# Weights as the moving operand: 512-column matmuls in gates and two output projections, merged matmuls in the input projection

## The chip, the cores and the metric

The kernel runs on one core of a Trainium2 chip. The metric is the device time of one execution in microseconds (us), as the median over several runs; lower is better. Engines are named as in the profile: PE (TensorE matmul), PEld (its weight loads), DVE (VectorE), ACT (ScalarE), POOL (GpSimd), SP (SyncE, which issues most DMAs).

## The reference

One layer of an encoder trunk over 256 tokens of 2048 channels in float32, and a last RMSNorm:

```
n  = rms_norm(h);  u = n @ w_in            # columns: q, kv, rope key | z, xBC, dt | gates g_attn, g_ssd
a  = mla(u) @ w_o_attn                     # 16 heads, rotary key, softmax over 256 keys
s  = rms_norm((y_f + y_b + d * xs) * silu(z)) @ w_o_ssd     # two scans in chunks of 128, 8 groups
m  = sigmoid(g_attn) * a + sigmoid(g_ssd) * s
h  = h + m @ w_out
h  = h + conv_ffn(rms_norm(h))             # up 2 x 5632, depthwise conv over 3, gate, down
out = rms_norm(h)
```

xBC goes through a depthwise convolution over five tokens and a silu before the scans.

## The kernel before

Everything lies transposed on the chip: channels in the 128 partitions, the 256 tokens in the free dimension. The weights are cut into slabs of 128 output channels by 16 blocks of 128 input channels (1 MB each). A slab is one *job*: SP loads it into one of three `raw` buffers (`load`, L128), and each half of it (eight blocks) is split by ACT and DVE into a rounded part `wh` and a rest `wl` (`split_to`, L139 and L140), in one of HB=5 buffers each. PE multiplies the parts with the activations, which are split in the same way (hi and lo, in one page with hi in row 0 and lo in row 1), and sums over the blocks in a PSUM bank. There are four banks (`gps`, tile `g`) for the jobs and four (`sps`, tile `s`) for the rest.

Two forms of the products exist. `mm3` (L145 to L147) makes three matmuls for each block, each with 256 moving columns (the tokens) and each with its own weight load. `dense(..., merge=True)` (L165, L166) makes two: `wh` against hi and lo at once, 512 columns, into both halves of a bank, and `wl` against hi, 256 columns, into the first half:

```
if merge:
    pe.matmul(ps, lhsT=wh[:, b, :], rhs=x, start=k == 0, stop=False)
    pe.matmul(ps[:, 0, :], lhsT=wl[:, b, :], rhs=x[:, 0, :], start=False, stop=k == ktot - 1)
else:
    mm3(ps, wh[:, b, :], wl[:, b, :], x[:, 0, :], x[:, 1, :], k == 0, k == ktot - 1)
```

The halves of a merged bank are then added by `halves_sum` (an ACT copy, L178, and a DVE add, L179). A third form stands in `v_job` (L509 to L511) alone: the activations are the stationary operand (128 tokens by 128 channels) and four weight blocks side by side the moving one, 512 columns.

The jobs run in the order in which they are appended: ten of the input projection (`win`) for the attention's latents, the rope key and dt; the attention's jobs (R, V, QK) with 16 gate slabs (`ga_job`) strewn among them; 16 slabs of `w_o_attn` (`oa_evac`); for each of eight groups B, C, four x and four z slabs of the input projection with one or two gate slabs (`gate_s`); six gate slabs; 32 jobs of `w_o_ssd`, two for each of 16 output slabs (`os_evac`); 16 of `w_out`; and the feed-forward part. Small pieces of work (rope, softmax, the scans `ssd_*`) are hung before jobs by `at(slot, ...)`. The input projection's slabs other than gates (`win` with merge=False) use `mm3`; gates, `w_o_attn`, `w_o_ssd` but for its last slab, and nearly all that follows are merged.

What is done with a finished bank: the convolved slabs (`conv5`) read it with one ACT operation (L621) and four DVE operations (L624) and end in a silu (L625); z slabs with one ACT silu (L648); gates with `halves_sum` and a tanh (L598).

Of the kernel before, what the change touches and what calls it, by code (L numbers as in the profile page):

```python
# [8 lines left out]
F32 = mybir.dt.float32  # L9
# [6 lines left out]
P = 128  # L16
S = 256
# [30 lines left out]
class Job:  # L48


    def __init__(self, src, nb, mm, evac):
        self.src, self.nb, self.mm, self.evac = src, nb, mm, evac
        self.sides, self.post = [], []
        self.whole = None


@with_exitstack
def tile_bidir_hybrid_layer(ctx: ExitStack, tc, xT, pos, vec, cst, w_in, w_r, w_v, w_qk, w_oa,
# [23 lines left out]
    def f32(ap):  # L82
        return ap.bitcast(F32)
# [17 lines left out]
    def vcol(name, i=0):  # L101
        o = VOFF[name] + i
        return V[:, o:o + 1]
# [29 lines left out]
    def split_to(n):  # L133
        while hptr[0] < min(n, len(halves)):
            i, h, nb = halves[hptr[0]]
            r = raws[i][:, 8 * h:8 * h + nb, :]
            wh = wp.tile([P, 8, P], F32R, tag="wh", bufs=HB, name="wh")
            wl = wp.tile([P, 8, P], F32R, tag="wl", bufs=HB, name="wl")
            act.activation(wh[:, :nb, :], r, AF.Copy)  # L139
            dve.tensor_sub(wl[:, :nb, :], r, f32(wh[:, :nb, :]))  # L140
            hl[hptr[0]] = (wh, wl)
            hptr[0] += 1

# [5 lines left out]
    def dense(src, nb, get, evac, cell=None, k0=0, ktot=None, merge=True):  # L149

        cell = {} if cell is None else cell
        ktot = nb if ktot is None else ktot

        def mm(h, n, wh, wl):
            if k0 == 0 and h == 0:
                cell["ps"] = gpsum([P, 2, S] if merge else [P, S])
            ps = cell["ps"]  # L160
            for b in range(n):
                k = k0 + 8 * h + b
                x = get(k)
# [11 lines left out]
        return j  # L175

    def halves_sum(ps, o):
        act.activation(o, ps[:, 1, :], AF.Copy)  # L178
        dve.tensor_add(o, o, ps[:, 0, :])  # L179
# [150 lines left out]
    def lat_evac(which, m):  # L330
        def ev(ps):
            if m == 0:
                lat[which] = page([P, 4, S], name=which)
                lat[which + "s"] = p1(name=which + "s")
            sq = lat[which + "s"] if m == 0 else p1(name="sq1")
            act.activation(lat[which][:, m, :], ps, AF.Copy)
            act.activation(sq, ps, AF.Square)
            if m:
                dve.tensor_add(lat[which + "s"], lat[which + "s"], sq)
        return ev  # L340
# [102 lines left out]

    def kr_evac(ps):
        t = p1((P, 1, S), name="krf")
        act.activation(t[:, 0, :], ps, AF.Copy)
        dts["krf"] = (t, swapped(t, 1))

    def kr_rope():
# [139 lines left out]

    ta, ts_ = {}, {}  # L590

    def gate_evac(store, m):
        def ev(ps):
            if m % 4 == 0:
                store[m // 4] = page([P, 4, S], name="gate")
            t = store[m // 4][:, m % 4, :]
            halves_sum(ps, t)
            act.activation(t, t, AF.Tanh, scale=0.5)  # L598
        return ev

    mixD = dr.tile([4, P, 4, S], F32, name="mixD")

    def oa_evac(m):
        def ev(ps):
            t = ta[m // 4]
            o = p1(name="oa")
            halves_sum(ps, o)
            dve.scalar_tensor_tensor(t[:, m % 4, :], t[:, m % 4, :], 1.0, o, ALU.add, ALU.mult)
            if m % 4 == 3:
                nc.sync.dma_start(mixD[m // 4], t)  # L610
        return ev


    class Grp:
# [3 lines left out]
    ssd_ss = {}  # L618

    def conv5(ps, cb, o):  # L620
        act.activation(o, ps, AF.Identity, scale=vcol("cw", 2 * 48 + cb), bias=vcol("cb", cb))  # L621
        for k, a, b in ((0, slice(2, S), slice(0, S - 2)), (1, slice(1, S), slice(0, S - 1)),
                        (3, slice(0, S - 1), slice(1, S)), (4, slice(0, S - 2), slice(2, S))):
            dve.scalar_tensor_tensor(o[:, a], ps[:, b], vcol("cw", k * 48 + cb), o[:, a], ALU.mult, ALU.add)  # L624
        act.activation(o, o, AF.Silu)  # L625

    def bc_evac(g, which):
# [138 lines left out]
    def ssd_r():  # L766
        r_ssd["t"] = rsqrt_tok(token_sums([ssd_ss["a"][:, b, :] for b in range(2)]), 4096)

    def ssd_r2():
        ps = spread(r_ssd["t"])  # L770
        r_ssd["r"] = p1(name="r_ssd")
        act.activation(r_ssd["r"], ps, AF.Copy)

    def ssd_split(g):
        for b in range(2):
            t = page([P, 2, 2, S], F32R, name="yHL")
# [5 lines left out]
                                         ALU.mult, ALU.subtract)  # L782
            yHL[2 * g + b] = t

    mixS, mHL = {}, {}

    def mix_load(q):
        mixS[q] = page([P, 4, S], name="mixS")
        nc.sync.dma_start(mixS[q], mixD[q])

    def os_evac(m):
        def ev(ps):
            t = ts_[m // 4][:, m % 4, :]
            o = p1(name="ms")
            sum_times(ps, r_ssd["r"], o)
            dve.scalar_tensor_tensor(o, t, 1.0, o, ALU.add, ALU.mult)
            dve.tensor_add(o, o, mixS[m // 4][:, m % 4, :])
            if m % 2 == 0:
                mHL[m // 2] = page([P, 2, 2, S], F32R, name="mHL")
            hi, lo = mHL[m // 2][:, 0, m % 2, :], mHL[m // 2][:, 1, m % 2, :]  # L800
            act.activation(hi, o, AF.Copy)
            dve.tensor_sub(lo, o, f32(hi))
        return ev


    hp, hHL = {}, {}
# [99 lines left out]

    win_i = [0]

    def win(evac, st=nHL, merge=False):
        j = dense(w_in[win_i[0]], 16, lambda k: pair(st, k), evac, merge=merge)  # L910
        win_i[0] += 1
        return j
# [4 lines left out]
        late.append((slot, lambda: fn(*a)))  # L917

    for m in range(4):
        win(lat_evac("q", m), xHL)  # L920
    for m in range(4):
        win(lat_evac("kv", m), xHL)
    win(kr_evac)
    win(dt_evac)
    at(2, emit_xsq)
# [20 lines left out]
    at(50, dt_rows)  # L946

    ga = [0]

    def ga_job():  # L950
        win(gate_evac(ta, ga[0]), merge=True)
        ga[0] += 1


# [34 lines left out]
    for it in "g R0 g g g V0 QK0 g QK1 V1 QK2 g QK3 V2 R1 g QK4 g QK5 V3 QK6 g QK7 g g g g g".split():  # L989
# [5 lines left out]
            Vj(int(it[1]))  # L995
        else:
            QK(int(it[2]))
    for m in range(16):
        dense(w_oa[m], 16, lambda k: pair(oT, k), oa_evac(m))
        if ga[0] < 16:  # L1000
            ga_job()
    gs = [0]

    def gate_s(n):
        for _ in range(n):
            win(gate_evac(ts_, gs[0]), merge=True)
            gs[0] += 1
    for g in range(G):
        b = len(jobs)
# [23 lines left out]
    for g in range(G):  # L1033
        at(b - 4 + g + (2 if g > 6 else 0), ssd_split, g)
    at(b + 5, ssd_r)
    at(b + 6, ssd_r2)
    b = len(jobs)
    for m in range(16):
        cell = {}
        dense(w_os[m, 0], 16, lambda k: pair(yHL, k), os_evac(m), cell, 0, 32, m < 15)  # L1040
        dense(w_os[m, 1], 16, lambda k: pair(yHL, k), os_evac(m), cell, 16, 32, m < 15)
    for q in range(4):
        at(b + 8 * q - (1 if q else 0), mix_load, q)
    b = len(jobs)
    for m in range(16):
# [163 lines left out]
```

## Time and profile before

| | |
|---|---|
| median of three runs | 1993.49 us (1992.39 to 1993.75) |
| the profiled execution | 1994.73 us, of which the trace spans 1992.9 us |
| busy share | PE 99%, PEld 91%, DVE 74%, ACT 60% |
| granted TensorE clock, mean | 0.997 of full speed |
| from HBM | 371.91 MB read, mean 190 GB/s |

The busy time of PE counts a matmul from its start to its end, and matmuls overlap; so the distance between the starts of two matmuls tells what one costs, and not its duration. In the rows a line of the timeline gives start (us), duration (us), engine, line, operation, the tile written and those read, and the shape.

### The profile page before, as it was taken

Reading aid. Unit: us, or ns where it says so; the run is one execution under the profiler, and the core shown is the slowest. Engines: PE = TensorE matmul, PEld = TensorE weight load, DVE = VectorE, ACT = ScalarE, POOL = GpSimd, SP = SyncE. Lnnn points to the kernel's source line nnn. Section 1 sums busy time; section 2 is a strip of 40 time slices with the busy share of each in tenths; the row PEclk is TensorE's granted clock in tenths of the full one; section 3 lists DMA queues with packets and bytes.
Section 4 is the critical chain, followed back from the end, with each engine's and each line's share of the span. In section 5 each row is a group of like instructions: output and inputs, shape, how many; then the busy total and the mean of one; then the engine's idle time right before and its main releaser. Section 6 shows DMA issues by size and latency. Waiting matters only on the chain.

```text
span 1992.9 us, 32794 instructions
## 1 busy us (share of the span) xinstructions
PE 1979.4 (99%) x13204; PEld 1810.8 (91%) x13204; DVE 1471.3 (74%) x2374; ACT 1205.5 (60%) x1894; POOL 0.2 (0%) x4
## 2 busy tenths in 40 slices
PE   9999999999999999999999999999999999999997
PEld 9999988999999999999888988888888888888886
DVE  7977766768877977887756676888756777567775
ACT  6666544677878788785644445655434555335564
POOL 0000000000000000000000000000000000000000
PEclk9999999999999999999999999999999999999998
DMA  7544356666556555644556555555555555555553
GB/s 270 180 172 156 132 176 218 239 208 205 172 206 226 181 184 207 227 171 170 187 201 211 200 210 201 187 191 189 182 184 189 190 189 181 182 189 190 185 159 122
DMA packets 58425, 379.54 MB, mean 190 GB/s; under 512 B 6816, under 2 KB 7456, under 8 KB 17568
## 3 DMA queue, kind: packets, MB, share of 16 engines
q1 hardware_dynamic: 56592, 375.08, 54.1%
q10 hardware_dynamic: 1680, 2.37, 0.4%
q8 instruction: 103, 1.69, 0.3%
q14 instruction: 50, 0.41, 0.1%
HBM read 371.91 MB, written 4.33 MB: 189 GB/s over the span
## 4 chain that ended last, share of the span: by engine, by line
PE 97%; DVE 2%; DMA 0%; ACT 0%; issue 0%; ACTq 0%; SPq 0%; DVEq 0%
PE g L165 41%; PE g L166 21%; PE g L147 10%; PE g L146 10%; PE g L145 10%; PE s L727 1%; PE s L736 1%; PE s L147 0%; PE s L145 0%; PE s L146 0%; DVE wl L140 0%; PE s L709 0%; PE s L570 0%; DVE xHL L232 0%; DMA x<-in_xT 0%; PE g L509 0%
## 5 line engine op out<-in xcount | busy, mean ns | idle before, releaser
L139 ACT ACTIVATE wh<-raw 128x1024 fp32r<-128x1024 f32 (+1 forms) x670 | 700.7, 1048 | 677.2 <-PE g L165 533.6
L140 DVE TENSOR_TENSOR wl<-raw,wh 128x1024 fp32r<-128x1024 f32 (+1 forms) x670 | 808.3, 1210 | 403.8 <-ACT wh L139 395.3
L165 PE MATMUL g<-hHL,wh 128*128 128x512 f32 x1360 | 477.6, 397 | 0.0
L145 PE MATMUL g<-xHL,wh 128*128 128x256 f32 x1424 | 405.1, 285 | 0.0
L147 PE MATMUL g<-xHL,wl 128*128 128x256 f32 x1424 | 403.5, 283 | 0.9 <-DVE wl L140 0.9
L146 PE MATMUL g<-xHL,wh 128*128 128x256 f32 x1424 | 403.6, 283 | 0.2 <-DVE xHL L232 0.2
L166 PE MATMUL g<-hHL,wl 128*128 128x256 f32 x1360 | 381.9, 281 | 0.0
L165 PEld LDWEIGHTS g<-hHL,wh 128*128 128x128 f32 x1360 | 255.3, 188 | 60.6
L147 PEld LDWEIGHTS g<-xHL,wl 128*128 128x128 f32 x1424 | 272.1, 191 | 1.1 <-DVE wl L140 1.1
L146 PEld LDWEIGHTS g<-xHL,wh 128*128 128x128 f32 x1424 | 272.2, 191 | 0.4 <-DVE xHL L232 0.4
L145 PEld LDWEIGHTS g<-xHL,wh 128*128 128x128 f32 x1424 | 272.1, 191 | 0.4
L166 PEld LDWEIGHTS g<-hHL,wl 128*128 128x128 f32 x1360 | 257.5, 189 | 0.0
L165 PE MATMUL g<-aHL,wh 128*128 128x512 f32 x692 | 244.8, 399 | 0.0
L166 PE MATMUL g<-aHL,wl 128*128 128x256 f32 x692 | 194.0, 281 | 0.0
L165 PE MATMUL g<-xHL,wh 128*128 128x512 f32 x512 | 182.0, 399 | 0.0
L165 PE MATMUL g<-yHL,wh 128*128 128x512 f32 x480 | 166.5, 392 | 0.0
L165 PEld LDWEIGHTS g<-aHL,wh 128*128 128x128 f32 x692 | 130.1, 188 | 32.6 <-DVE aHL L866 0.6
L166 PE MATMUL g<-xHL,wl 128*128 128x256 f32 x512 | 143.6, 281 | 0.0
L166 PE MATMUL g<-yHL,wl 128*128 128x256 f32 x480 | 134.6, 280 | 0.0
L166 PEld LDWEIGHTS g<-aHL,wl 128*128 128x128 f32 x692 | 131.0, 189 | 0.1
L165 PEld LDWEIGHTS g<-xHL,wh 128*128 128x128 f32 x512 | 96.3, 188 | 22.5
L165 PEld LDWEIGHTS g<-yHL,wh 128*128 128x128 f32 x480 | 89.8, 187 | 19.5
(296 smaller groups left out, 2748.2 us busy)
## 6 DMA issues: line engine op xcount, KB each, us to landing
raw<-in_w_in SPq DMA_DIRECT2D x120, 1024.0 KB, 4.9
raw<-in_w_up SPq DMA_DIRECT2D x88, 1024.0 KB, 4.8
raw<-in_w_os SPq DMA_DIRECT2D x32, 1024.0 KB, 4.8
raw<-in_w_dn SPq DMA_DIRECT2D x32, 1024.0 KB, 5.0
raw<-in_w_oa SPq DMA_DIRECT2D x16, 1024.0 KB, 4.8
FB<-acsD SPq DMA_DIRECT2D x32, 512.0 KB, 7.3
raw<-in_w_out SPq DMA_DIRECT2D x16, 1024.0 KB, 4.8
raw<-in_w_dn SPq DMA_DIRECT2D x16, 768.0 KB, 4.2
```

The costliest lines, as they stand in the source:

```text
L139: act.activation(wh[:, :nb, :], r, AF.Copy)
L140: dve.tensor_sub(wl[:, :nb, :], r, f32(wh[:, :nb, :]))
L145: pe.matmul(ps, lhsT=wH, rhs=xH, start=first, stop=False)
L146: pe.matmul(ps, lhsT=wH, rhs=xL, start=False, stop=False)
L147: pe.matmul(ps, lhsT=wL, rhs=xH, start=False, stop=last)
L165: pe.matmul(ps, lhsT=wh[:, b, :], rhs=x, start=k == 0, stop=False)
L166: pe.matmul(ps[:, 0, :], lhsT=wl[:, b, :], rhs=x[:, 0, :], start=False, stop=k == ktot - 1)
L727: pe.matmul(px[j0][:, b, c * P:(c + 1) * P], lhsT=q.xw[:, 1 - c, js], rhs=q.cX[:, 1 - c, :], start=True, stop=True)
L736: pe.matmul(ps[j0][64 * hh:64 * hh + 64, b, c * P:(c + 1) * P], lhsT=q.xt[:, c, h * 64:h * 64 + 64], rhs=q.F[c][:, h, :], start=True, stop ...
```

## The change

All of it moves work between forms of the same products.

1. **Quads.** The 32 gate slabs, the 16 slabs of `w_o_attn` and the 32 jobs of `w_o_ssd` become quads, in the manner of `v_job`. A quad is four slabs side by side; a unit of it is one job and takes four blocks of each of the four slabs, by four DMAs of 2 KB rows instead of one of 8 KB rows. It makes 24 matmuls of 512 columns. A quad's two banks (one for each 128 tokens) are held from its first unit to its last, 4 units (8 for `w_o_ssd`) later; the units stand where the slabs stood. Results have tokens in the partitions: gates take one tanh for each bank, `w_o_attn` one DVE operation, `w_o_ssd` an ACT copy that scales by `r_ssd` and two DVE operations (`ssd_r2`, which spread `r_ssd` over partitions, goes).
2. **Back to channels.** `mix_channels` turns the mixed result of a quad back by eight PE transposes, and splits it into `mHL`. The first two slabs of `w_out` are cut into halves of eight blocks, so that the last quad's transposes can stand behind their first halves.
3. **Merge.** The other slabs of the input projection, except the very first one, are merged. Their evacuations gain a `halves_sum`, in `conv5` through a new tile `cu`.

```diff
+        elif j.quad:
+            tq = t.rearrange("p (m k) c -> p m k c", m=4)
+            for m, src in enumerate(j.src):
+                nc.sync.dma_start(tq[:, m], src)
...
+            if jobs[i].quad:
+                r = raws[i].rearrange("p (m k) c -> p m k c", m=4)[:, :, 2 * h:2 * h + 2, :]
+                vh, vl = (w.rearrange("p (k m) c -> p m k c", k=2) for w in (wh, wl))
...
+    def quad(src, q, kt, get, evac):
...
+            def mm(h, n, wh, wl):
+                if u == 0 and h == 0:
+                    cell["ps"] = [gpsum([P, 512]), gpsum([P, 512])]
+                wH, wL = (w.rearrange("p (k m) c -> p k (m c)", k=2) for w in (wh, wl))
+                for kk in range(2):
+                    k = 4 * u + 2 * h + kk
+                    x = get(k)
+                    for t in range(2):
+                        ts = slice(t * P, (t + 1) * P)
+                        ps = cell["ps"][t]
+                        pe.matmul(ps, lhsT=x[:, 0, ts], rhs=wH[:, kk, :], start=k == 0, stop=False)
+                        pe.matmul(ps, lhsT=x[:, 0, ts], rhs=wL[:, kk, :], start=False, stop=False)
+                        pe.matmul(ps, lhsT=x[:, 1, ts], rhs=wH[:, kk, :], start=False, stop=k == kt - 1)
...
-        dve.tensor_scalar(v, ps, vcol("dtb"), None, ALU.add)
+        act.activation(v, ps[:, 1, :], AF.Identity, bias=vcol("dtb"))
+        dve.tensor_add(v, v, ps[:, 0, :])
...
+    def gate_evac(store):
...
+            act.activation(store[q][:, t, :], ps, AF.Tanh, scale=0.5)
...
     def conv5(ps, cb, o):
-        act.activation(o, ps, AF.Identity, scale=vcol("cw", 2 * 48 + cb), bias=vcol("cb", cb))
+        u = p1(name="cu")
+        halves_sum(ps, u)
+        act.activation(o, u, AF.Identity, scale=vcol("cw", 2 * 48 + cb), bias=vcol("cb", cb))
...
-            act.activation(grp[g].z[:, j, :], ps, AF.Silu)
+            z = grp[g].z[:, j, :]
+            halves_sum(ps, z)
+            act.activation(z, z, AF.Silu)
...
+    def os_evac(q, t, ps):
...
+        act.activation(o, ps, AF.Copy, scale=r_ssd["t"][:, t:t + 1])
+        dve.scalar_tensor_tensor(o, ts_[q][:, t, :], 1.0, o, ALU.add, ALU.mult)
+        dve.tensor_add(o, o, mixS[q][:, t, :])
+
+    def mix_channels(q):
+        for i in range(2):
+            ps = spsum([P, 2, S])
+            for b in range(2):
+                for t in range(2):
+                    m = 2 * i + b
+                    pe.transpose(ps[:, b, t * P:(t + 1) * P], mixT[q][:, t, m * P:(m + 1) * P], ident)
+            v = mHL[2 * q + i] = page([P, 2, 2, S], F32R, name="mHL")
+            act.activation(v[:, 0], ps, AF.Copy)
+            dve.tensor_sub(v[:, 1], ps, f32(v[:, 0]))
...
-    def win(evac, st=nHL, merge=False):
+    def win(evac, st=nHL, merge=True):
...
-        win(lat_evac("q", m), xHL)
+        win(lat_evac("q", m), xHL, m > 0)
...
+        jobs += quad(lambda m: OsSrc(m), q, 32, lambda k: pair(yHL, k), os_evac)
+        at(len(jobs) + (1 if q < 3 else 2), mix_channels, q)
...
+    for h in range(2):
+        for m in range(2):
+            dense(w_out[m][:, 8 * h:8 * h + 8, :], 8, lambda k: pair(mHL, k), wo_evac(m), cells[m], 8 * h, 16)
```

## Rows read from the trace of the kernel before

**Rows 1.** The page: busy time by engine with its share of the span; the granted clock in 40 slices; the chain of work that ended last, by engine and by line.
```profile
PE 1979.4 (99%) x13204; PEld 1810.8 (91%) x13204; DVE 1471.3 (74%) x2374; ACT 1205.5 (60%) x1894; POOL 0.2 (0%) x4
...
PEclk9999999999999999999999999999999999999998
...
PE 97%; DVE 2%; DMA 0%; ACT 0%; issue 0%; ACTq 0%; SPq 0%; DVEq 0%
PE g L165 41%; PE g L166 21%; PE g L147 10%; PE g L146 10%; PE g L145 10%; PE s L727 1%; PE s L736 1%; PE s L147 0%; PE s L145 0%; PE s L146 0%; DVE wl L140 0%; PE s L709 0%; PE s L570 0%; DVE xHL L232 0%; DMA x<-in_xT 0%; PE g L509 0%
```

**Rows 2.** The waits: who waited for whom, us in total, times, longest us.
```profile
ACT wh L139 <- PE g L165: 533.6, 397, 2.1
DVE wl L140 <- ACT wh L139: 395.3, 396, 5.8
...
ACT wh L139 <- DMA raw<-in_w_in: 2.1, 4, 1.3
...
PEld g L147 <- DVE wl L140: 1.9, 2, 1.1
```

**Rows 3.** The timeline of PE: the first matmul of three unmerged slabs in a row (48 matmuls each), and the first matmul after the third.
```profile
370.95 0.28 PE L145 MATMUL g<-xHL,wh 128*128 128x256 f32 x1
...
388.22 0.28 PE L145 MATMUL g<-xHL,wh 128*128 128x256 f32 x1
```

**Rows 4.** The timeline of PE: the first matmul of five merged slabs of w_o_attn in a row (32 matmuls each), which end where rows 3 begin; the first of one merged gate slab and the first after it; the first of 27 merged jobs of w_o_ssd in a row, and the first after them.
```profile
343.22 0.39 PE L165 MATMUL g<-oT,wh 128*128 128x512 f32 x1
...
406.22 0.40 PE L165 MATMUL g<-xHL,wh 128*128 128x512 f32 x1
...
411.87 0.28 PE L145 MATMUL g<-xHL,wh 128*128 128x256 f32 x1
...
978.21 0.39 PE L165 MATMUL g<-yHL,wh 128*128 128x512 f32 x1
...
1127.97 0.39 PE L165 MATMUL g<-yHL,wh 128*128 128x512 f32 x1
```

**Rows 5.** The timeline of PE: a V job, 24 matmuls of 512 moving weight columns: the first, the 12th, and the first matmul of the job behind it.
```profile
99.69 0.39 PE L509 MATMUL g<-wh,latH 128*128 128x512 f32 x1
...
102.21 0.39 PE L511 MATMUL g<-wh,latL 128*128 128x512 f32 x1
...
...
105.16 0.28 PE L145 MATMUL g<-latH,wh 128*128 128x256 f32 x1
```

**Rows 6.** The timeline of PE: eight transposes and the matmul behind them; then the spreading of r_ssd (L210, four instructions) inside a merged pair.
```profile
560.82 1.04 PE L709 MATMUL s<-CT,xs 128*128 128x128 f32 x8
561.61 0.37 PE L145 MATMUL g<-xHL,wh 128*128 128x256 f32 x1
...
968.39 0.40 PE L165 MATMUL g<-yHL,wh 128*128 128x512 f32 x1
968.63 0.61 PE L210 MATMUL s<-dg,ones 128*128 128x128 f32 x4
...
969.19 0.40 PE L165 MATMUL g<-yHL,wh 128*128 128x512 f32 x1
```

**Rows 7.** Groups of instructions by line: operation, tiles, shapes, count | busy us, mean ns of one | idle time before them and what ended it.
```profile
L621 ACT ACTIVATE xs<-g,V 128x256 f32<-128x256 f32 x32 | 17.6, 550 | 0.2
...
L179 DVE TENSOR_TENSOR gate<-gate,g 128x256 f32<-128x256 f32 x32 | 13.3, 416 | 3.6 <-ACT gate L178 3.6
L598 ACT ACTIVATE gate<-gate 128x256 f32<-128x256 f32 x32 | 13.3, 414 | 14.7 <-DVE gate L179 14.7
...
L648 ACT ACTIVATE sz<-g 128x256 f32<-128x256 f32 x32 | 11.9, 373 | 0.1
...
L178 ACT ACTIVATE gate<-g 128x256 f32<-128x256 f32 x32 | 11.7, 367 | 3.0 <-issue 1.6 <-PE g L166 0.9 <-DVE yHL L781 0.6
L750 DVE TENSOR_TENSOR y<-y,yx 128x512 f32<-128x512 f32 x16 | 10.9, 683 | 0.0
...
L710 ACT ACTIVATE xt<-s 128x512 f32<-128x512 f32 x16 | 8.6, 590 | 0.0
```

**Rows 8.** Busy time by engine in one group of the SSD stage, and in the first and the last part of it.
```profile
504.50:573.20 68.70, 68.70 (x576) 67.67 (x575) 55.41 (x101) 56.41 (x94) 0.00 (x0) 1.00 0.58 200
...
515.00:550.00 35.00, 35.00 (x279) 34.26 (x278) 34.44 (x66) 29.00 (x53) 0.00 (x0) 1.00 0.51 179
550.00:573.20 23.20, 23.20 (x196) 23.20 (x195) 16.28 (x27) 17.03 (x29) 0.00 (x0) 1.00 0.80 272
```
The columns are: stretch, its length, then busy us (and instructions) of PE, PEld, DVE, ACT, POOL, granted clock, DMA share, GB/s.

**Rows 9.** The timeline of DVE and PE in that group: two splits in a row, of which the first ends near 533.4; the first read of a convolved slab's bank by DVE (L624); the start of the half for which the first of the two splits was made (the k-th split belongs to the k-th half, counted through the trace), which is also the start of the second job after that slab.
```profile
532.19 2.35 DVE L140 TENSOR_TENSOR wl<-raw,wh 128x1024 fp32r<-128x1024 f32 x2
534.46 0.47 DVE L624 SCALAR_TENSOR_TENSOR xs<-g,V,xs 128x254 f32<-128x254 f32 x1
...
537.88 0.28 PE L145 MATMUL g<-xHL,wh 128*128 128x256 f32 x1
```

**Rows 10.** DMA issues: tiles, count, KB each, median us from issue to landing; then the timeline: one issue of a slab of w_o_ssd, and ACT's first read of that slab.
```profile
raw<-in_w_os SPq DMA_DIRECT2D x32, 1024.0 KB, 4.8
...
out<-h SPq DMA_DIRECT2D x2, 256.0 KB, 2.5
...
1000.11 0.33 SPq L128 DMA_DIRECT2D raw<-in_w_os  x1
...
1011.62 1.06 ACT L139 ACTIVATE wh<-raw 128x1024 fp32r<-128x1024 f32 x1 [1.70 <-PE g L165]
```

More of the change, by code (lines that the diff above doesn't have):

```diff
@@ L54, in __init__ @@
         self.whole = None
+        self.quad = False
 @with_exitstack
@@ L175, in dense, with unit, ev, __init__ @@
         return j
+    def quad(src, q, kt, get, evac):
+        cell = {}
+        def unit(u):
+            def mm(h, n, wh, wl):
[11 more added lines that the diff above has]
+                        pe.matmul(ps, lhsT=x[:, 1, ts], rhs=wH[:, kk, :], start=False, stop=k == kt - 1)
+            def ev():
+                if 4 * u + 4 == kt:
+                    for t in range(2):
+                        evac(q, t, cell["ps"][t])
+            j = Job([src(4 * q + m)[:, 4 * u:4 * u + 4, :] for m in range(4)], 16, mm, ev)
+            j.quad = True
+            return j
+        return [unit(u) for u in range(kt // 4)]
+    class OsSrc:
+        def __init__(self, m):
+            self.m = m
+        def __getitem__(self, i):
+            k = i[1].start
+            return w_os[self.m, k // 16][:, k % 16:k % 16 + 4, :]
     def halves_sum(ps, o):
@@ L335, in ev @@
             sq = lat[which + "s"] if m == 0 else p1(name="sq1")
-            act.activation(lat[which][:, m, :], ps, AF.Copy)
-            act.activation(sq, ps, AF.Square)
+            o = lat[which][:, m, :]
+            if len(ps.shape) == 2:
+                act.activation(o, ps, AF.Copy)
+            else:
+                halves_sum(ps, o)
+            act.activation(sq, o, AF.Square)
             if m:
@@ L590, in tile_bidir_hybrid_layer, with ev, oa_evac @@
     ta, ts_ = {}, {}
[L592 to L598, printed above, removed]
-        return ev
[L601 to L611, printed above, removed]
+    def gate_evac(store):
+        def ev(q, t, ps):
+            if t == 0:
+                store[q] = page([P, 2, 512], name="gate")
+            act.activation(store[q][:, t, :], ps, AF.Tanh, scale=0.5)
+        return ev
+    mixD = dr.tile([4, P, 2, 512], F32, name="mixD")
+    def oa_evac(q, t, ps):
+        g = ta[q]
+        dve.scalar_tensor_tensor(g[:, t, :], g[:, t, :], 1.0, ps, ALU.add, ALU.mult)
+        if t == 1:
+            nc.sync.dma_start(mixD[q], g)
     class Grp:
@@ L948, in tile_bidir_hybrid_layer @@
     ga = [0]
+    GS_AT = [10 + 16]
+    gs_blocks = []
+    for g in range(G):
+        for f, n in ((0, 6), (1, 4)):
+            GS_AT[0] += n
+            gs_blocks += [GS_AT[0] + i for i in range(GS_IN[g][f])]
+            GS_AT[0] += GS_IN[g][f]
+    gs_blocks += [GS_AT[0] + i for i in range(16 - len(gs_blocks))]
+    ga_units = [u for q in range(4) for u in quad(lambda m: w_in[10 + m], q, 16, lambda k: pair(nHL, k),
+                                                  gate_evac(ta))]
+    gs_units = [u for q in range(4) for u in quad(lambda m: w_in[gs_blocks[m]], q, 16, lambda k: pair(nHL, k),
+                                                  gate_evac(ts_))]
     def ga_job():
-        win(gate_evac(ta, ga[0]), merge=True)
+        jobs.append(ga_units[ga[0]])
+        win_i[0] += 1
         ga[0] += 1
@@ L997, in tile_bidir_hybrid_layer @@
             QK(int(it[2]))
[L998 to L1001, printed above, removed]
+    for q in range(4):
+        for u in quad(lambda m: w_oa[m], q, 16, lambda k: pair(oT, k), oa_evac):
+            jobs.append(u)
+            if ga[0] < 16:
+                ga_job()
     gs = [0]
@@ L1005, in gate_s @@
         for _ in range(n):
-            win(gate_evac(ts_, gs[0]), merge=True)
+            jobs.append(gs_units[gs[0]])
+            win_i[0] += 1
             gs[0] += 1
@@ L1035, in tile_bidir_hybrid_layer @@
     at(b + 5, ssd_r)
-    at(b + 6, ssd_r2)
     b = len(jobs)
[L1038 to L1041, printed above, removed]
+    for q in range(4):
+        jobs += quad(lambda m: OsSrc(m), q, 32, lambda k: pair(yHL, k), os_evac)
+        at(len(jobs) + (1 if q < 3 else 2), mix_channels, q)
     for q in range(4):
@@ L1044, in tile_bidir_hybrid_layer @@
     b = len(jobs)
-    for m in range(16):
+    cells = [{}, {}]
+    for h in range(2):
+        for m in range(2):
+            dense(w_out[m][:, 8 * h:8 * h + 8, :], 8, lambda k: pair(mHL, k), wo_evac(m), cells[m], 8 * h, 16)
+    for m in range(2, 16):
         dense(w_out[m], 16, lambda k: pair(mHL, k), wo_evac(m), merge=m < 15)
```

39 lines of the change are left out of this document (14 added, 25 removed).

## The prediction

> **What bounds the kernel now.** I read the page first. PE is busy for 99% of the span, the chain that ended last is PE for 97%, and its clock is at the higher of its two levels (2.4 GHz) in nearly every slice [rows 1]; so a busy share can't rise, and the clock has nothing to give. The waits come second: ACT and DVE wait for PE (ACT 533.6 us for a weight buffer), while PE waited for a split 1.9 us in all and ACT for a slab's DMA 2.1 us [rows 2]. So PE's own instruction stream sets the time almost everywhere, and a change is worth what it takes out of that stream, as long as it makes no new wait.
>
> Durations on PE overlap, so the third view is the timeline, read by starts. All three forms stream the same number of columns: for one block of one slab 3 x 256 unmerged, 512 + 256 merged, and in a V job 24 x 512 for 16 blocks of one slab's worth, each time 12288 columns a job. At 2.4 GHz that is 5.12 us. What a job takes above that goes with the number of matmuls:
>
> - unmerged, 48 matmuls: (388.22 - 370.95) / 3 = 5.757 us, 120 ns a matmul [rows 3];
> - merged, 32 matmuls: 411.87 - 406.22 = 5.65 us for the gate slab, but (1127.97 - 978.21) / 27 = 5.547 us in w_o_ssd and (370.95 - 343.22) / 5 = 5.546 us in the last slabs of w_o_attn [rows 3, 4]. One form has two spacings, and I don't see what chooses;
> - V, 24 matmuls: 105.16 - 99.69 = 5.47 us; from the 12th on (105.16 - 102.21) / 13 = 0.227 us a matmul, which is 5.45 us a job [rows 5].
>
> **The change part by part.** *Gates as quads.* A unit is 24 matmuls of 512 columns with the operands placed as in a V job, so I price it by that row. Gate units stand singly between other jobs, so they get the whole V job, start included: 32 x (5.65 - 5.47) = 5.8 us gained. If gates had run at the short spacing it would be 2.5; if units run settled, 6.4.
>
> *w_o_attn as quads.* Rows 4 show slabs of that stage at 5.546 and a gate at 5.65; I take 5.60 before and the settled 5.45 after, since units follow each other: 16 x 0.15 = 2.4 us (bounds 1.2 and 3.3).
>
> *w_o_ssd as quads.* 30 merged jobs at 5.547 and two unmerged at 5.757 become 32 at 5.446: 3.0 + 0.6 = 3.6 us (with 5.47: 2.9).
>
> *Input projection merged.* 89 slabs (q without its first, kv, rope key, dt, and ten in each of eight groups). By the gate slab, which reads the same activations amid the same slabs, 89 x (5.757 - 5.65) = 9.5 us. By the short spacing it would be 89 x 0.21 = 18.7 us. I take the lower end, because the row nearest in place and operand is the gate's, and keep the upper for a rival.
>
> A row against a page: each matmul above shows some 13 ns beyond its columns (120 against 106.7; 227 against 213.3) [rows 3, 5]. The Trainium skill, "TensorE: Matmul & The Clock Gate", section on the back-to-back issue gap, gives N / 2.4 + 2.5 ns for matmuls one after another at the full clock. By it an estimate of all that quads and merging save would be about 5 us in place of 21.3, and little would be left after the transposes. The rows have the spacing itself in this kernel, so the sum goes by them.
>
> *Taken away on PE:* the spreading of r_ssd stretches one pair to 969.19 - 968.39 = 0.80 us, where a pair takes 5.547 / 16 = 0.35: 0.45 us gained [rows 4, 6]. *Added on PE:* 32 transposes. Eight take 561.61 - 560.82 = 0.79 us [rows 6], so four times that: 3.2 us lost.
>
> *Do the transposes wait?* Behind a quad's last matmul come an ACT copy (0.59 us) and for each 128 tokens two DVE operations of 512 columns (0.683 each) [rows 7]: 0.59 + 4 x 0.683 = 3.3 us. One unit of 5.45 us stands in between (two half slabs of w_out for the last quad). Nothing, then, up to 2 us of queueing. The last quad's transposes are followed by four blocks (1.4 us) that use older pages, against 0.59 + 0.683 = 1.3 us for the new page: 0 to 1 us.
>
> *ACT and DVE.* They are off the path, but they fill the buffers. In most stages the change relieves them: a gate slab loses 0.367 + 0.414 us of ACT and 0.416 of DVE and gets a quarter of two tanh of some 0.59 [rows 7]. In the SSD stage they get more. A group adds ten halves_sum: on DVE 10 x 0.416 less one gate's, +3.7 us; on ACT six copies of 0.367, four z slabs at +0.41 (0.367 + 0.414 - 0.373), less 0.5 for the gate, +3.3 us [rows 7]. Of a period of 68.7 us DVE has 55.41 and ACT 56.41 [rows 8]; after, 59.1 and 59.7 of 67.4, or 88% and 89%. That fits, but not evenly: from 515 to 550 DVE is busy 34.44 of 35 us [rows 8]. Six of the ten additions (2.5 us) fall there. The cover is the distance from a finished split to its use: 537.88 - 533.4 = 4.5 us [rows 9]. About five additions (2.1 us) and PE's own gain (5 x 0.107 us) come off, and 1.9 us are left. From 550 on DVE has 6.9 us idle to catch up.
>
> *Banks.* A quad holds two of the four g banks from its first unit to its last, and the gate quads are drawn over the SSD stage at one unit a group. So the slabs there rotate through two banks in place of four: a slab's bank must be free when the second job after it starts. The DVE's first read of one slab's bank starts at 534.46; when the new addition stands there, the bank is free at 534.9, and that job starts at 537.88 [rows 7, 9]: 3.0 us early. The trace thus has the evacuation hidden with two banks. The Trainium skill speaks against taking banks away: "Perfetto Trace Analysis", section Optimizing Tensor Performance, asks that independent groups of matmuls rotate through different PSUM banks so that the evacuation of one overlaps the next. By the row the sum loses nothing; by the rule, if the overlap breaks, it loses what the second rival below gives.
>
> *DMAs.* A quad's slab comes in four issues of 256 KB with 2 KB rows. One slab lands in 4.8 us; a store of 256 KB with 2 KB rows took 2.5 us, so a slab takes between 4.8 and, all four in series, 10.0. The load is issued 1011.62 - 1000.11 = 11.5 us before ACT reads it [rows 10]. Nothing; beyond that cover each us late would be a us of PE in up to 80 jobs.
>
> For the small waits that the thinner covers may leave (SSD stage, transposes, start-up) I put 1.5 us, with bounds 0 and the rivals below.
>
> **Sum.** 5.8 + 2.4 + 3.6 + 9.5 + 0.45 - 3.2 - 1.5 = 17.05 us gained. The profiled execution took 1994.73 us, which gives 1977.7; it is 1.24 us above the median shown, so for a median I expect 1993.49 - 17.05 = 1976.4 us.
>
> **Rivals.**
> 1. *Merged slabs at the short spacing.* For: w_o_ssd and the end of w_o_attn have it [rows 4]. Against: the gate, the nearest row, has not. 9.2 us more: 1967.2.
> 2. *Two banks are too few* (slower). In the saturated stretch the new addition waits behind other DVE work: two splits (2.35 us, rows 9) and the 2.5 us of new additions ahead of it make 4.85, against 3.0 us of cover: PE stands 1.85 us. At two slabs of each of eight groups that is 30 us: 2006. It decides from 1.15 slabs a group (17.05 / 8 / 1.85). Against: a bank is done with after one short DVE operation, where DVE read it four times before.
> 3. *Splits come late.* If ACT's new copies (6 x 0.367 = 2.2 us) stand in series with DVE's 2.5 us and PE's own 0.6, cover falls by 5.3 of 4.5 us: 0.8 us a group, 6.4 in all: 1983. For: both engines above 85%. Against: they work side by side.
> 4. *The spacing belongs to the place and not to the form.* One merged form differs by 0.10 us a job between two places, as much as unmerged and merged differ side by side [rows 3, 4]. Then merging and gate quads give nothing, and 2.4 + 3.6 + 0.45 - 3.2 - 1.5 = 1.75 us are left: 1991.7, no change. Against: in the SSD stage the two forms stand next to each other, each with its own. The page's formula above points the same way.
>
> **How the numbers follow.** Forecast 0.60, rival 1 0.15, rival 3 0.12, rival 2 0.08, rival 4 0.05. The time is the forecast's, 1976.5. The range 1964 to 1987 holds the first three with the bounds of the terms (short spacing also in w_out, settled units, or waits up to 10 us); what it leaves out is rivals 2 and 4 and tails. A measurement tells a change from none from about 0.2% on, 4 us: faster 0.85 (forecast, rival 1, most of rival 3), same 0.07 (rival 4, part of rival 3), slower 0.08 (rival 2).
>
> **What the new profile would show.** Quad matmuls 227 ns apart with no more than 235; slabs of the SSD stage 5.55 to 5.65 us from start to start; PE still at 99% with waits for `wl` of a few us at most; a group of the SSD stage about 67.4 us long; eight transposes in 0.8 us with no idle time of PE before them. Wrong it would be if PE waits for g banks or for `wl` in each group, if groups stay at 68.7 us or grow, if DVE or ACT passes 95% over a group, if `raw` lands later than its use, or if the jobs behind w_o_ssd, which are not changed, move to the other spacing (0.1 us a job, either way).

## The result, and the profile after

The changed kernel takes 1975.92 us (median of four runs, 1974.66 to 1977.09), against 1993.48 us for the kernel before in runs beside it: a ratio of 0.9913, 95% interval 0.9896 to 0.993. That is 17.6 us less. The forecast was 1976.5 and faster. The profiled execution took 1974.66 us with a span of 1972.9, so 20.0 us of span went, where the working expected 17.05. That is more than the medians show, because the four executions fall at 1974.7 and 1977.1, two each, and the traced one is the shortest of them, while the trace of the kernel before (1994.73 us) is longer than all its other executions. The sum came out right, but not every term.

The page of the changed kernel (busy time by engine, granted clock by slice, chain that ended last):

```profile
PE 1956.5 (99%) x11136; PEld 1702.4 (86%) x11136; DVE 1466.5 (74%) x2349; ACT 1208.5 (61%) x1892; POOL 0.2 (0%) x4
...
PEclk9999999999999999999999999999999999999999
...
PE 93%; DVE 3%; ACT 2%; issue 1%; DMA 1%; SPq 0%; DVEq 0%; ACTq 0%
```

Against [rows 1]: PE is at 99% as before, with 2068 instructions fewer. DVE and ACT hold the same total. What is new is in the chain of work that ended last, where DVE, ACT and DMA have 6% together and had 2%.

The waits of the changed kernel (who waited for whom, us in total, times, longest): ACT's first row, then PE's first and its row for splits:

```profile
ACT wh L150 <- PE g L176: 433.1, 342, 2.5
...
PE g L176 <- DVE cu L229: 2.0, 2, 1.1
...
PE g L177 <- DVE wl L151: 0.8, 1, 0.8
```

ACT waits for PE and splits are hardly ever late, as in [rows 2]. The second row is new: twice, PE waits for a g bank that DVE is still reading for a `cu` (the new sum of two halves in `conv5`).

Quads on the timeline of PE in w_o_ssd: the first matmul of a quad and the one behind it, the end of its first unit with the eight transposes of the quad before, and the first matmul of the next quad:

```profile
993.61 0.39 PE L204 MATMUL g<-wh,yHL 128*128 128x512 f32 x1
993.83 0.39 PE L205 MATMUL g<-wl,yHL 128*128 128x512 f32 x1
...
998.82 0.39 PE L206 MATMUL g<-wh,yHL 128*128 128x512 f32 x1
999.05 1.03 PE L853 MATMUL s<-CT,ms 128*128 128x128 f32 x8
999.84 0.48 PE L204 MATMUL g<-wh,yHL 128*128 128x512 f32 x1
...
1038.05 0.39 PE L204 MATMUL g<-wh,yHL 128*128 128x512 f32 x1
```

A unit takes 999.05 - 993.61 = 5.44 us, 227 ns a matmul, from its first matmul on. The transposes cost 999.84 - 999.05 = 0.79 us, and no idle time stands before them.

The next table is worked out from the traces: the time from the start of a stage's job to the start of the next job, summed over the stage, in us (what lies ahead of the first job and behind the last is left out). Its last four columns are experiments, told below.

```
                              before   after   merge    quads    cut      two
                                               alone    alone    columns  banks
latents, rope key, dt (9)       56.5    53.7    53.7     56.0     53.4     53.8
attention gates (16)           105.3   103.5   106.2    102.7    108.2    111.6
R, V, QK                       103.2   103.7   104.4    103.1    104.0    110.5
w_o_attn (16)                   91.4    89.2    91.4     89.2     94.0     94.9
B and C slabs (16)             119.3   116.9   116.6    119.3    116.9    116.6
x slabs (32)                   190.1   190.1   187.2    191.3    194.0    192.1
SSD gates (16)                  95.1    92.1    94.8     92.7     96.8     94.6
z slabs (32)                   191.3   186.1   186.3    191.2    185.8    185.8
w_o_ssd (32)                   178.4   176.8   178.4    176.8    186.8    178.4
w_out                           90.6    90.1    90.6     91.6     90.1     90.6
feed-forward                   744.9   743.8   743.8    743.8    744.9    744.9
span                          1992.9  1972.9  1979.7   1984.3   2002.8   2001.0
```

A job's time holds the small work hung before the next job, so a piece that moves by one job shifts some tenths between rows; and in a few places the matmuls of two neighbouring jobs stand mixed. The x slabs stand out: 32 of them were merged and their stage gained nothing.

Busy time in the SSD stage after: an ordinary group, one with a wait for a bank, and the saturated stretch of rows 8 (columns as in [rows 8]):

```profile
495.51:562.64 67.13, 67.13 (x408) 58.68 (x407) 58.46 (x111) 59.43 (x105) 0.00 (x0) 1.00 0.59 204
562.64:631.39 68.75, 67.66 (x409) 58.79 (x408) 57.77 (x105) 59.14 (x102) 0.00 (x0) 1.00 0.59 200
515.00:550.00 35.00, 35.00 (x195) 30.21 (x195) 34.64 (x71) 28.26 (x52) 0.00 (x0) 1.00 0.59 209
```

A group of 68.70 us is now 67.13, and DVE and ACT hold 87% and 89% of it. From 515 to 550 DVE is full (34.64 of 35 us) and PE still never idle. In the second row PE is 1.09 us short of its stretch, and that is the new wait.

### The profile page after: what moved, and what is told of

It reads as the page before. It is cut to its first block, busy times and chain, and to the rows that moved or that the text cites. A ratio compares the mean times of both kernels' runs of the same rounds, so it can differ in the third digit from the quotient of the medians.

```text
span 1972.9 us, 29057 instructions
## 1 busy us (share of the span) xinstructions
PE 1956.5 (99%) x11136; PEld 1702.4 (86%) x11136; DVE 1466.5 (74%) x2349; ACT 1208.5 (61%) x1892; POOL 0.2 (0%) x4
## 4 chain that ended last, share of the span: by engine, by line
PE 93%; DVE 3%; ACT 2%; issue 1%; DMA 1%; SPq 0%; DVEq 0%; ACTq 0%
PE g L176 41%; PE g L177 21%; PE g L204 7%; PE g L206 7%; PE g L205 7%; PE g L158 1%; PE g L157 1%; PE g L156 1%; DVE wl L151 1%; ACT wh L150 1%; PE s L780 1%; PE s L157 0%; PE s L789 0%; DVE bcf L675 0%; PE s L158 0%
## 5 line engine op out<-in xcount | busy, mean ns | idle before, releaser
L176 PE MATMUL g<-xHL,wh 128*128 128x512 f32 x1424 | 503.7, 398 | 2.0 <-DVE cu L229 2.0
L177 PE MATMUL g<-xHL,wl 128*128 128x256 f32 x1424 | 399.8, 281 | 0.8 <-DVE wl L151 0.8
L176 PEld LDWEIGHTS g<-xHL,wh 128*128 128x128 f32 x1424 | 267.3, 188 | 65.7 <-issue 1.2
L204 PE MATMUL g<-wh,xHL 128*128 128x512 f32 x256 | 100.1, 392 | 0.0
L204 PE MATMUL g<-wh,yHL 128*128 128x512 f32 x256 | 99.8, 390 | 0.0
L206 PE MATMUL g<-wh,xHL 128*128 128x512 f32 x256 | 99.8, 390 | 0.0
L205 PE MATMUL g<-wl,xHL 128*128 128x512 f32 x256 | 99.8, 390 | 0.0
L206 PE MATMUL g<-wh,yHL 128*128 128x512 f32 x256 | 99.6, 389 | 0.0
L205 PE MATMUL g<-wl,yHL 128*128 128x512 f32 x256 | 99.6, 389 | 0.0
L901 DVE SCALAR_TENSOR_TENSOR uc<-u,V,uc 128x255 f32<-128x255 f32 x176 | 84.7, 481 | 4.6 <-ACT uc L899 1.5
L176 PE MATMUL g<-mHL,wh 128*128 128x512 f32 x240 | 83.6, 392 | 0.0
```

Source lines behind the costliest of these rows:

```text
L204: pe.matmul(ps, lhsT=x[:, 0, ts], rhs=wH[:, kk, :], start=k == 0, stop=False)
L205: pe.matmul(ps, lhsT=x[:, 0, ts], rhs=wL[:, kk, :], start=False, stop=False)
L206: pe.matmul(ps, lhsT=x[:, 1, ts], rhs=wH[:, kk, :], start=False, stop=k == kt - 1)
L901: dve.scalar_tensor_tensor(o[:, a], u[:, b], vcol("fcw", k * 88 + cb), o[:, a], ALU.mult, ALU.add)
```

## The experiments

The theory going in: PE's matmul stream is the bound; each form has its own price, so the parts add up; the rotation of the g banks is the weak place. Against it stood: that the columns alone set the time and the gain comes from elsewhere (transposes, evacuations); and that loads or transposes eat part of it.

**Merge alone.** The kernel before with `merge=True` in `win` (all but the first slab) and the evacuations that go with it; no quads.

```diff
-    def win(evac, st=nHL, merge=False):
+    def win(evac, st=nHL, merge=True):
```

> The kernel before with the merge of the input projection alone (89 slabs of 48 matmuls become 32), no quads. Theory (a job costs its columns plus a price for each matmul, and PE is the bound): 89 x 0.107 = 9.5 us less than before, 1984, slabs of the SSD stage at 5.65 us. Rival short spacing: 89 x 0.21 = 18.7 us less, 1975. Rival place (spacing belongs to the stage): no change, slabs stay at 5.76. With four banks for the slabs no waits of PE for a g bank are expected.

Measured: 1982.91 us (1981.52 to 1984.65), ratio 0.9945 (0.9932 to 0.9957): 11.0 us less. In the table the latents gain 2.8 (but 0.9 turns up again in the gates behind them, and 1.2 in R, V and QK, where one wait of PE for a split is 1.5 us), B and C gain 2.7, x 2.9, z 5.0: 11.3 us net, where the prediction had 9.5 for merging.

**Quads alone.** The changed kernel with the input projection unmerged, and its evacuations as before.

```diff
-    def win(evac, st=nHL, merge=True):
+    def win(evac, st=nHL, merge=False):
```

> The changed kernel with the input projection unmerged as before: quads alone. Theory: 5.8 + 2.4 + 3.6 + 0.45 - 3.2 = 9 us less than before, 1984.5, less about 1 us of small waits; the two parts then add up to the whole change. Rival place: quads of w_o_attn and w_o_ssd alone would gain, less the transposes: 2 us or less, 1991.5.

Measured: 1985.73 us (1984.79 to 1986.54), ratio 0.9959 (0.9947 to 0.9972): 8.2 us less. The two parts sum to 19.2, the whole change gave 17.6: some 1.6 us would be lost where they meet, which is less than the intervals of the ratios can tell apart. The table says where to look: x slabs gain 2.9 with merging alone, and nothing in the whole change. With quads alone they lose 1.2, and there too PE waits once for a bank (0.5 us, for one that `conv5` still reads).

**Columns cut.** The changed kernel with each 512-column matmul of a quad made as two of 256, save the first into each bank: 1888 matmuls more, the same columns, banks, loads and evacuations.

```diff
-                        pe.matmul(ps, lhsT=x[:, 0, ts], rhs=wL[:, kk, :], start=False, stop=False)
...
+                        for w, l, r in ((0, 0, wH), (1, 0, wL), (2, 1, wH)):
+                            first = k == 0 and w == 0
+                            for c in ((0, 512),) if first else ((0, 256), (256, 512)):
+                                pe.matmul(ps[:, c[0]:c[1]], lhsT=x[:, l, ts], rhs=r[:, kk, c[0]:c[1]], start=first,
+                                          stop=k == kt - 1 and w == 2 and c[1] == 512)
```

> The changed kernel with each 512-column matmul of a quad cut into two of 256 columns (all but the first of each bank), so same operands, same loads, same evacuation, same columns, twice the matmuls. Theory (price of some 13 ns for each matmul): a unit goes from 5.45 back to 5.76 us, 80 x 0.31 = 25 us more than the changed kernel, 2001, slower than before. Rival (what gains is the operands' roles, the lighter evacuation or the loads, and not the number of matmuls): 1976, as the changed kernel.

Measured: 2004.88 us (2004.49 to 2006.14), ratio 1.0058 (1.0042 to 1.0073), 29.0 us above the changed kernel. The timeline of PE in this kernel, the matmuls that end two quads of w_o_ssd:

```profile
1061.44 0.64 PE L207 MATMUL g<-wh,yHL 128*128 128x256 f32 x3
...
1108.37 0.64 PE L207 MATMUL g<-wh,yHL 128*128 128x256 f32 x3
```

and in the changed kernel the two that answer to them:

```profile
1037.83 0.39 PE L206 MATMUL g<-wh,yHL 128*128 128x512 f32 x1
...
1082.24 0.39 PE L206 MATMUL g<-wh,yHL 128*128 128x512 f32 x1
```

A quad grows from 44.41 to 46.93 us, with 190 matmuls more: 13.2 ns for each. Over the four quad stages of the table it is 24.2 us for 1888, 12.8 ns. So the number of matmuls is what the forms differ in, columns being equal; the rest of the 29 us is mainly 3.9 us in the x slabs. Every matmul here has a weight load of its own (the page above counts 11136 of each), and the cut added as many of the one as of the other; so which of the two the 13 ns belong to is not shown. The Trainium skill, "TensorE: Matmul & The Clock Gate", section on the back-to-back issue gap, gives 2.5 ns beyond the columns for a matmul by itself, and says that in a stream of weight loads and matmuls both set the spacing. 1888 times 2.5 ns would be an estimate of 4.7 us; the measured price in this stream is five times that.

**Five banks.** The changed kernel with one more bank for the jobs and one fewer for the rest.

```diff
-    gps = ctx.enter_context(tc.tile_pool(name="gps", bufs=4, space=bass.MemoryType.PSUM))
-    sps = ctx.enter_context(tc.tile_pool(name="sps", bufs=4, space=bass.MemoryType.PSUM))
+    gps = ctx.enter_context(tc.tile_pool(name="gps", bufs=5, space=bass.MemoryType.PSUM))
+    sps = ctx.enter_context(tc.tile_pool(name="sps", bufs=3, space=bass.MemoryType.PSUM))
```

> The changed kernel with five PSUM banks for g and three for s in place of four and four, so a slab rotates through three banks while a gate quad holds two. Theory: PE's waits for the addition into cu go (2 us as named, some 3 us with the long jobs around them), 1973, unless the scans wait for an s bank. Rival (the two long jobs have another cause): 1976 or more.

Measured: 1973.81 us (1972.84 to 1974.43), ratio 0.9899 (0.9886 to 0.9913). What PE waited for here, the first four rows:

```profile
PE s L1159 <- DVE epsc L100: 1.0, 1, 1.0
PE g L177 <- DVE wl L151: 0.9, 1, 0.9
PE s L260 <- DVE dg L259: 0.9, 1, 0.9
PE s L780 <- DVE yx L798: 0.7, 3, 0.3
```

The waits for `cu` are gone, and the x slabs take 186.9 us in place of 190.1. So a bank more for the jobs gives the x slabs their gain back. The medians differ by 2.1 us, but the intervals of the two ratios overlap, and B and C slabs came out 1.5 us longer and the feed-forward part 1.1: the net gain isn't resolved. The fourth row is the other side of the exchange: the scans (`ssd_y`, which fill four s banks) now wait for an s bank until DVE has read it (`yx`), as the expectation had allowed for. These waits stand in B and C jobs and make 0.7 of their 1.5 us.

How the wait comes about is seen on the timeline of the changed kernel, ACT, DVE and PE where an x slab of the fourth group waits; the last two lines are the ends of the two other long jobs, in the fifth and the seventh group:

```profile
583.37 0.40 PE L176 MATMUL g<-xHL,wh 128*128 128x512 f32 x1
...
586.33 0.42 ACT L676 ACTIVATE bcf<-bcf 128x256 f32<-128x256 f32 x1 [1.82 <-DVE bcf L675]
586.66 1.05 ACT L150 ACTIVATE wh<-raw 128x1024 fp32r<-128x1024 f32 x1
587.61 0.40 ACT L683 ACTIVATE bcH<-bcf 128x256 fp32r<-128x256 f32 x1
588.02 1.28 ACT L727 ACT_TABLE_LOAD   x1
589.32 1.06 ACT L727 ACTIVATE FB<-FB 128x1024 f32<-128x1024 f32 x1
590.28 0.64 ACT L228 ACTIVATE cu<-g 128x256 f32<-128x256 f32 x2
590.68 0.75 DVE L229 TENSOR_TENSOR cu<-cu,g 128x256 f32<-128x256 f32 x2
591.25 0.47 PE L176 MATMUL g<-xHL,wh 128*128 128x512 f32 x1 [1.06 <-DVE cu L229]
...
658.38 0.38 PE L157 MATMUL s<-bcL,bcH 128*128 128x256 f32 x1 [0.33 <-DVE bcL L684]
...
794.48 0.47 PE L176 MATMUL g<-xHL,wh 128*128 128x512 f32 x1 [0.99 <-DVE cu L229]
```

The bank wanted at the end is that of the slab which ended at 583.37. Its evacuation, an ACT copy (L228) and a DVE add (L229), starts 6.9 us later: on ACT it stands behind a silu that waited 1.82 us for DVE, a split, a rounding, a table load of 1.28 and an exponential of 1.06. Two of the four banks belong to the open gate quad, so the second job after it has none. The job that started at 583.37 therefore lasts 591.25 - 583.37 = 7.88 us, where the same job of most other groups lasts 6.38. Two such jobs (7.88 and 7.52) make 2.6 us. A third long one (6.97, 0.6 over) is no bank: there a product of the scan itself waits 0.33 us for `bcL`, the low part of a B or C slab, and with merging alone, where no quad holds a bank, the same job took 6.76.

**No transposes.** The changed kernel with `mHL` split from the mixed result as it stands; the eight transposes of each quad, 32 in all, are left out, and channels are in the wrong order.

```diff
-                    pe.transpose(ps[:, b, t * P:(t + 1) * P], mixT[q][:, t, m * P:(m + 1) * P], ident)
+            ps = mixT[q][:, i, :].rearrange("p (b s) -> p b s", b=2)
```

> The changed kernel without the 32 transposes back to channels: mHL is taken straight from mixT, so w_out multiplies data in the wrong order, with all shapes, splits and evacuations kept. Theory (eight transposes cost PE 0.79 us and hide nothing else): 3.2 us less than the changed kernel, 1972.7, and the w_o_ssd stage 176.8 - 2.4 = 174.4 us by the trace. Rival (the transposes wait for the quad's evacuation, so their place costs more than their length): 5 us less or more. Rival (they fill gaps): no change.

Measured: 1972.51 us (1971.86 to 1973.2), ratio 0.9896 (0.9879 to 0.9912): 3.4 us below the changed kernel; but the intervals of the two ratios overlap, so the trace has to carry it. There w_o_ssd, where three of the four sets stand, gains 2.7 (176.8 to 174.1), which is 0.9 us a set: the 0.79 of the row and 0.1 more in the unit behind it. The price of 3.2 is near. In w_out, where the fourth set stands, the stage came out 0.4 us longer, because its slabs of 32 matmuls ran at 5.65 us here and at 5.55 in the changed kernel.

**One load.** A quad's unit laid out so that one DMA of 8 KB rows brings it, in place of four of 2 KB rows.

```diff
-            for m, src in enumerate(j.src):
-                nc.sync.dma_start(tq[:, m], src)
+            nc.sync.dma_start(t, j.src)
```

> The changed kernel with the weights of the quads laid out in DRAM so that a unit is one load of 1 MB with rows of 8 KB, in place of four loads of 256 KB with rows of 2 KB. Theory (the load has 11.5 us of cover and lands well before): no change, 1976 within 1.5 us. Rival (short rows delay splits somewhere): 2 us or more less, and ACT's waits for raw shrink.

Measured: 1976.18 us (1975.19 to 1977.29), ratio 0.9913 (0.9898 to 0.9928): no change. The DMA totals of the changed kernel, then of this one:

```profile
DMA packets 93260, 379.32 MB, mean 192 GB/s; under 512 B 10688, under 2 KB 11328, under 8 KB 62912
```

```profile
DMA packets 58696, 379.27 MB, mean 192 GB/s; under 512 B 6848, under 2 KB 7488, under 8 KB 18112
```

The 34,564 packets more of the changed kernel cost nothing that shows: its 256 KB issues land 3.5 to 4.0 us after they are made (medians by tile), and the cover in the kernel before was 11.5 [rows 10].

**Two banks without quads.** Merge alone, with `bufs=2` in place of 4 for the jobs throughout: the second rival at full strength.

> The kernel before with the input projection merged (no quads) and two PSUM banks for g in place of four, all through. Theory (second rival of the prediction in small: an evacuation that comes late makes PE wait where only two banks are left): waits of PE for the additions into cu and for evacuations of the attention's jobs appear, the slabs x of the SSD stage take 190 us or more where the same kernel with four banks took 187.2, and the time is 3 to 10 us above that kernel's 1983. Rival (two banks are enough everywhere): 1983, x at 187.

Measured: 2003.01 us, one run, 20.1 above merge alone. What PE waited for here, the first three rows:

```profile
PE g L514 <- DVE gate L179: 4.0, 1, 4.0
PE g L165 <- DVE cu L179: 3.5, 4, 1.1
PE s L145 <- ACT qk L537: 2.9, 1, 2.9
```

By the table x slabs lose 4.9 us against merge alone, but the attention part 15.0 (gates 5.4, R, V and QK 6.1, w_o_attn 3.5, with the small work between them): more than I expected, and mostly not where I had put it. The Trainium skill, "Perfetto Trace Analysis", section Optimizing Tensor Performance, asks for a rotation through banks so that evacuation overlaps; the run agrees and prices it: 20 us where two banks are all there is, against 2.6 us in two of eight groups where a quad holds the other two.

**Nudges.** The changed kernel with one idle transpose hung before each fourth job of the later feed-forward part (26 in all).

```diff
+    def nudge():
+        pe.transpose(spsum([P, P]), ident, ident)
+    for i in range(b + 33, len(jobs), 4):
+        at(i, nudge)
```

> The changed kernel with one idle transpose (128 columns, result unused) before every fourth job of the feed-forward part from its 33rd job on, 26 in all; their own length is some 0.11 us each, 3 us. Theory (which of the two spacings a merged stream keeps is a phase that it falls into, and not the place): some stretches of the jobs that ran at 5.65 us move to 5.55, and the time is between 1969 and 1979 as more or fewer do. Rival (the spacing belongs to the place, the operands or the buffers): all stay at 5.65, and the time is 1979.

Measured: 1973.63 us (1973.09 to 1974.05), ratio 0.99 (0.9885 to 0.9915): work was added, and the time did not rise. The timeline of PE in this kernel, first matmuls of merged up jobs, two apart in each pair:

```profile
1542.47 0.39 PE L176 MATMUL g<-hHL,wh 128*128 128x512 f32 x1
...
1553.57 0.39 PE L176 MATMUL g<-hHL,wh 128*128 128x512 f32 x1
...
1587.20 0.40 PE L176 MATMUL g<-hHL,wh 128*128 128x512 f32 x1
...
1598.50 0.40 PE L176 MATMUL g<-hHL,wh 128*128 128x512 f32 x1
```

One job is 5.55 us in the first pair and 5.65 in the second: same form, operand and stage. The four-job stretches between nudges run at 5.65, 5.65, 5.55, 5.55 and over again. So the spacing belongs neither to the form nor to the place. It is a state that a disturbance can change and that otherwise holds.

**Down projection as quads.** Five banks, and the feed-forward's down projection as quads too, with the last norm in token layout (32 transposes more): the change carried on.

```diff
+            jobs += quad(lambda m: w_dn[m][:, m0 * P:m1 * P].rearrange("p (k m) -> p k m", m=P), q, n,
+                         lambda k, m0=m0: pair(aHL, m0 + k), dn_evac(pi == 2))
```

> The kernel with five g banks, and the down projection made of quads as well: 48 jobs of 32 or 24 matmuls become 44 units of 24; h is turned to token layout by 32 transposes during the up projection, the last norm then scales by token, and the output leaves in token layout. The last up slab of each part is merged too. Theory: 48 slabs lose 32 x 0.2 + 16 x 0.07 = 7.5 us, the unmerged slabs and the waits for the last aHL 1 us, the end some 2 us (no spreading of the norm), against 3.2 us for transposes: about 7 us less than with five banks alone, 1966.5. Rival (the transposes or the pages make PE wait, or the merged stream of up falls into the longer spacing): 1971 or more.

Measured: 1967.78 us (1967.03 to 1968.31), ratio 0.987 (0.9856 to 0.9885): it beats both kernels. Jobs of the down projection take 239.6 us in place of 249.4 in the five-bank kernel, both counted to the end of the last matmul; the up projection takes 3.7 more, with its 32 transposes (3.2 at 0.79 for eight).

**Two nudges and four nudges.** The kernel just shown, with two (then four) idle transposes at the second up job of the second and the third feed-forward part, both of which ran at 5.65. I wanted a rule for the state: the count of matmuls, modulo four, ahead of a stretch.

```diff
+        for _ in range(2):       # 4 in the other
+            pe.transpose(spsum([P, P]), ident, ident)
+    for i in (b + 49, b + 97):
+        at(i, nudge)
```

> The kernel with the down projection in quads too, plus two idle transposes before the second up job of the second part and of the third. In that kernel all 56 jobs of these two parts ran at 5.65 us. Theory from the nudges (the spacing is a phase that goes by the count of matmuls: of four states two are long and two short, next to each other, so two extra matmuls always turn one into the other): both parts go to 5.55, 54 x 0.105 = 5.7 us less and 0.4 us for the transposes, 1962.5. Rival (the pattern was chance, or place): 5.65 stays, 1968.

> The same with four idle transposes in each place. Theory (four states): the phase comes back to where it was, all up jobs of the two parts stay at 5.65 us, 1968.5. Rival (any disturbance lets the stream fall into the shorter spacing): 5.55 in both, 1963.

Measured: with two, 1967.76 us (1967.05 to 1968.57), ratio 0.9871 (0.9854 to 0.9887): no change, and both parts stay at 5.65. With four, 1966.29 us in one run. The timeline of PE with four nudges, up jobs twenty apart, second part and then third part:

```profile
1497.72 0.40 PE L176 MATMUL g<-hHL,wh 128*128 128x512 f32 x1
...
1610.79 0.40 PE L176 MATMUL g<-hHL,wh 128*128 128x512 f32 x1
...
1766.08 0.39 PE L176 MATMUL g<-hHL,wh 128*128 128x512 f32 x1
...
1877.02 0.39 PE L176 MATMUL g<-hHL,wh 128*128 128x512 f32 x1
```

Second part 113.07 / 20 = 5.65, third part 110.94 / 20 = 5.55, after the same four nudges. My rule foretold a flip for two nudges and none for four. It fell both times, in both parts with two and in the third part with four. What selects the spacing stays open.

## Why the prediction was right, point by point

**What held.** PE's stream is the bound, and a form costs its columns and so much for each matmul: cutting the columns into smaller matmuls, with loads, banks and evacuations left in place, took back more than the whole gain. Quads run at 227 ns and the transposes at 0.79 us for eight. The w_o_ssd stage was to gain 3.6 + 0.45 - 2.4 (three of four sets of transposes) = 1.65 and gained 1.6. w_o_attn was to gain 2.4 and gained 2.2. Loads are covered. The group was to be 67.4 us with DVE 59.1 and ACT 59.7, and is 67.13 with 58.46 and 59.43.

**Gates, 5.8 forecast.** The two gate stages gained 1.8 + 3.0 = 4.8. The first gate job went from 5.63 to 6.38 us, because a piece of small work that stood with the dt slab now falls into it (as the latents' 2.8 shows from the other side). Without that job the gates gained 5.6: the term held.

**Merge, 9.5 forecast: too small.** Alone it is worth 11.3 us by the table and 11.0 by the medians. The working took the long spacing, 0.107 us a slab, for all 89. In fact B slabs and the last two z slabs of each group gained 0.2 each, as the short spacing would give (0.21 a slab), so that the 80 slabs of the SSD stage gained 0.13 on the mean. This is the step where one form had two spacings and I chose by the nearest row; the truth is a mixture, between that choice and rival 1.

**Small waits, 1.5 forecast: too small.** Two x slabs lost 2.6 us to banks, and the sum had put nothing for banks. It is rival 2 in small: right in its place (two banks, conv slabs), and only in part in its engine. I priced the queue on DVE, which had the least idle time, and the bank was late because ACT's copy stood in order behind other work of ACT, 6.9 us after the slab's end; of these, 1.82 us were ACT's own wait for DVE. The row that I used [rows 9] was of one group and of the DVE step; it does not show the stretches in which ACT loads a table and waits for DVE. The rival's price of 1.85 us a slab at two slabs in each group would have been 30; it was 1.5 and 1.1 us at two slabs in all.

**Not in the sum.** The feed-forward part gained 1.1 us and w_out 0.4 net of its transposes, by the spacing of merged jobs that were not changed (in w_out from 5.65 to 5.55 us); the prediction named that among its signs of being wrong, at 0.1 us a job, and the sum has no term for it. So the sum came out at 1976.4 through a merge that was worth more, and waits that cost more, than it said. That it met the median within 0.5 us is luck: terms were off by 1 us and more in both directions, and the four executions alone lie 2.4 us apart.

**Rivals.** Rival 3, late splits: the smallest distance from a finished split to its use in the SSD stage fell to 2.2 us (539.38 less the split's end at 537.13, worked out from the trace), against 1.9 forecast. PE's two waits for a split (0.8 and 0.6 us) stand at 16 and 104 us of the trace, ahead of the SSD stage, where it waited for none. Covers were thin and held. Rival 4, spacing of the place: merge alone and quads alone each gained, so the form has its price; but the nudges show that the extra 0.10 us of a merged job is indeed not the form's. Rival 1 came partly true, as said.

## What to carry to other kernels

Where PE's stream is the bound and columns are equal, count matmuls: in this kernel a form that moves 512 columns a weight load saved some 13 ns for each matmul, with its weight load, that it did away with, at the price of transposes that turn the result back. Count free PSUM banks over the time that an accumulation stays open, and look for the slowest evacuation on each engine in its queue order, not only on the busiest one. Before a price is taken from one row, look whether the same form has another elsewhere; where it has two, forecast a mixture.

## What the runs showed of the hardware that I had not expected

One price a matmul (its weight load with it) fits three forms at once. With 5.12 us of columns a job and 13.3 ns a matmul, 24, 32 and 48 matmuls should take 5.44, 5.546 and 5.76 us; measured are 5.44 (quads), 5.547 [rows 4] and 5.757 [rows 3].

Only the merged form, which alternates 512 and 256 columns, has a second, longer spacing, 5.65. It holds over tens of jobs and can flip at small disturbances, in either direction. In the kernel with down quads 56 of the 88 up jobs ran long, at 0.10 us each 5.6 us. What chooses it was not found. Quads never showed it.
